# Moving the second pair's index scores and its top-256 select to later places in three quarters of a sparse-attention layer

## The chip, the cores and the metric

The kernel runs on one core of one Trainium2 chip. TensorE (PE) multiplies matrices into PSUM, its weight loads are shown apart (PEld), VectorE (DVE), ScalarE (ACT) and GpSimd (POOL) work on vectors, SyncE (SP) issues the DMAs. The metric is the device time of one execution in microseconds (us), lower is better.

## The reference, cut to what matters

Three layers over 2048 tokens of width 1024. The first two (gated linear attention and spatial gating, then retention and pooling) are not touched. The change lies in the third: all tokens are projected, and then two branches run beside each other, a gated delta rule in chunks of 64 and an attention in which every token sees only 256 chosen tokens.

```python
proj = h @ w_in[layer]
(qkv_a, z_a, b_a, a_a, q_b, ckv, z_b, iq, ik, iw) = jnp.split(proj, list(SPLIT_OFFSETS), axis=-1)
o_a = gated_deltanet(qkv_a, z_a, b_a, a_a, ...)
o_b = dsa_sparse_attention(q_b, ckv, iq, ik, iw, ...)
mix = jnp.concatenate([o_a, o_b], axis=-1) @ w_out[layer]
x = x + gate[:, None, :] * rmsnorm(mix, g_post[layer])

# in dsa_sparse_attention, for each block of 128 queries
rel = jnp.einsum('bqhd,bsd->bqhs', iqb, ik)                 # 8 index heads
score = jnp.einsum('bqh,bqhs->bqs', iwb, jax.nn.relu(rel))
score = jnp.where(key_pos[None, None, :] <= t[None, :, None], score, -jnp.inf)
_, sel = lax.top_k(score, k_top)                            # k_top = 256
...
p = jax.nn.softmax(logits, axis=-1)                         # over the chosen keys, 4 heads
return jnp.einsum('bqhk,bqkr->bqhr', p, kv_sel)
```

## The kernel before

**The quarters.** `layer2` (L972) walks over four quarters `q` of 512 tokens, each of four blocks `b` of 128 queries; block `i = 4q + b` sees `n = 128 (i + 1)` keys. The blocks form two pairs, (0, 1) and (2, 3). In the first quarter (`q = 0`) the first pair needs no select, since it sees at most 256 keys.

**What a quarter does.** `begin` (L1111) transposes the rows `x` into the tiles `xh` and `xl` and makes the first projections. `chains` (L1189) makes the other 28 projections, numbered 0 to 27: 24 matmuls of 512 columns into a `pj` bank each. Numbers 0 to 3 are the index queries, 4 to 11 keys and queries of the delta rule (each followed by a convolution on VectorE), 12 to 15 its values (the same), 16 to 27 queries and gates (ScalarE alone takes them out). `index_scores` (L1339) makes the scores of a pair in steps: two matmuls into an `ix` bank (L1355, L1356), a relu on ScalarE (L1362) and a multiply-add on VectorE (L1363), eight heads for each 512 keys. `select` (L1368) finds the 256th largest score of each query of a pair. It has seven rounds, in each of which VectorE counts for one block (L1400) and ScalarE for the other (L1406), and some dozen tiny VectorE instructions set the next threshold from both; then a search among the candidates (L1473 to L1483), two more counts, a repair by match-replace (L1513), and the masks `jd`, `ja`. It ends with two branches on a loaded flag (`tc.If`, L1532) for rare cases. `attention` (L1573) takes the blocks in turn and four heads in each: `setup` (L1588) copies the block's mask into `mk`, `scores` (L1600) makes three matmuls for each 512 keys (L1619) and adds the mask on VectorE (L1621), then comes an exponential (L1627), transposes (L1640) and products (L1650). `delta` (L1827) is a serial recurrence over the quarter's four groups of 128 tokens. `output` (L1299) multiplies both branches by the output weights (L210) and writes the rows.

**What sets the order.** The streams are Python generators. `weave` (L1077) takes steps from them in proportion to the weight that stands beside each, and `part(stream, wait, n)` (L1093) lets a stream wait for some steps and then gives `n` of it. `PARTS` (L46) says at which projections a quarter's three weaves begin and `PACE` (L45) holds weights. I call the three weaves A, B and C, and the last one, with `output`, the tail:

- A: projections 4 to 11 (to 10 in the last two quarters) with the first pair's index scores.
- B: projections to 19 (to 18) with the second pair's index scores and the first pair's select.
- C: projections to 27 with the second pair's select, after 4 steps of wait 10 steps of attention, and after 20 steps 6 of delta.
- tail: the rest of delta and of attention, then `output`.

Up to the end of C, TensorE's instructions stand in just this order (`manual_schedule`, L1040). On the other engines, and on TensorE in the tail, a scheduler orders them by program order and readiness when the kernel is built; on the chip every engine works down its own fixed list. Nothing moves across a `tc.If` in VectorE's list.

**Buffers that the change touches.** `row8` (L859) hands out tiles of 2048 columns by tags with few buffers. Tag `xh` (2 buffers) serves `xh` and later the delta branch's result `mhA`, `mlA`; tag `rb` (2 buffers) serves the score rows of the second pair and later the attention's result `mhB`, `mlB`. `output` reads `mhA` and `mlA` for the first half of each sum, `mhB` and `mlB` for the second.

Of the kernel before, what the change touches and what calls it, by code (L numbers as in the profile page):

```python
# [22 lines left out]
P = 128  # L23
# [18 lines left out]
ORDERED = '@@'  # L42


PACE = [(6, 3, 30, 30, 10, 40, 20, 6)] * 4  # L45
PARTS = [(4, 12, 20), (4, 12, 20), (4, 11, 19), (4, 11, 19)]  # L46


def f(ap):
# [12 lines left out]
class Builder:  # L62
# [794 lines left out]
        return self.sb.tile([P, TB if dt == F32 else 4 * TB], dt, tag=tag, bufs=1, name=self.nm(tag))  # L857

    def row8(self, name, dt=F32):  # L859
        pair = {"xr": "ra", "P": "ra", "score01": "ra", "xh": "xh", "wq": "xh", "mhA": "xh", "mlA": "xh"}.get(name)  # L860
        if pair:
            return self.big.tile([P, 2048], dt, tag=pair, bufs=2, name=self.nm(name))
        if name in ("score23", "mhB", "mlB"):
            t = self.big2.tile([P, 2048 + 8], dt, tag="rb", bufs=2, name=self.nm(name))
            return t if name == "score23" else t[:, :2048]
        return self.big2.tile([P, 2048], dt, tag="r8", bufs=4, name=self.nm(name))
# [105 lines left out]
    def layer2(self, src, dst):  # L972
# [65 lines left out]
        for q in range(NQ):  # L1038
            pace = PACE[q]
            with self.tc.manual_schedule(engines={mybir.EngineType.PE}):  # L1040
                st = self.begin(q, xn)
                x = PARTS[q]
                for _ in self.chains(q, st, range(1, x[0])):
                    pass
                n = [8 * sum(-(-(4 * q + b + 1) // 4) for b in pair if 4 * q + b >= 2) for pair in ((0, 1), (2, 3))]
                self.weave((self.chains(q, st, range(x[0], x[1])), 8 * (x[1] - x[0]) + pace[0]), (self.index_scores(q, st, (0, 1)), n[0]))
                self.weave((self.chains(q, st, range(x[1], x[2])), 8 * (x[2] - x[1]) + pace[1]), (self.index_scores(q, st, (2, 3)), n[1]),
                           (self.select(q, st, (0, 1)), pace[2]))
                att, delta = self.attention(q, st), self.delta(q, st)
                n = [4 * (1 + -(-max(0, i - 1) // 4) + 2 * -(-(i + 1) // 4)) for i in range(4 * q, 4 * q + 4)]  # L1050
                self.dtag = "ix"
                m = 8 * (28 - x[2])
                self.weave((self.chains(q, st, range(x[2], 28)), m), (self.select(q, st, (2, 3)), pace[3]),
                           (self.part(att, 4, pace[4]), 4 + pace[4]), (self.part(delta, pace[6], pace[7]), pace[6] + pace[7]))
            self.dtag = "pj"
            self.weave((delta, 40 - pace[7]), (att, sum(n) - pace[4]))
            if q + 1 < NQ:
                xn = self.load_rows(q + 1, src)
            self.output(q, st)
# [513 lines left out]
    def attention(self, q, st):  # L1573
# [5 lines left out]
        blocks, split = {}, []  # L1579
# [8 lines left out]
        def setup(b):  # L1588
            i = 4 * q + b
            n = (i + 1) * P  # L1590
            if b in st["masks"]:
                for u in range(0, n, 512):
                    m = min(512, n - u)
                    nc.scalar.activation(mk[:, u:u + m], st["masks"][b][:, u:u + m], AF.Copy, scale=-BIG)
            else:
                nc.gpsimd.memset(mk[:, :n], 0.0)
                nc.gpsimd.affine_select(out=mk[:, i * P:n], in_=mk[:, i * P:n], pattern=[[-1, P]], base=0, channel_multiplier=1,
                                        compare_op=ALU.is_ge, fill=-BIG)
# [103 lines left out]
        order = [(b, h) for b in range(4) for h in range(4)]  # L1702
        queries(0)
        setup(0)
        yield
        lag = 2 if q < 2 else 1
        for t, (b, h) in enumerate(order + [(4, h) for h in range(lag)]):
            streams = []
            if t >= lag:
                streams.append((values(*order[t - lag]), 2 * -(-(4 * q + order[t - lag][0] + 1) // 4)))  # L1710
            if b < 4:
                streams.append((scores(b, h), 3 * (1 + -(-max(0, 4 * q + b - 1) // 4))))
            if h == lag and b > 0:
                streams.append((after(b - 1), 3))
            yield from self.woven(*streams)
            if h == 2 and b < 3:
                queries(b + 1)
            if h == 3 and b < 3:
                setup(b + 1)
# [338 lines left out]
```

## Time and profile before

| what | before |
|---|---|
| median of 3 runs | 3370.99 us (3364.59 to 3376.85) |
| the profiled execution's own time | 3370.53 us |
| its span, first to last instruction | 3368.8 us |
| granted TensorE clock, mean | 0.971 |
| busy: PE, DVE, ACT, POOL | 94%, 57%, 36%, 32% |

The span is 1.7 us shorter than the execution's time; sums below are made against 3370.53 us. The third layer takes the second half of the span, from about 1648 us. [...] A busy TensorE is no TensorE at its peak: a matmul is counted from issue to its modelled end, so the spacing of matmuls is the better price.

### The profile page before, as it was taken

The numbers are of one execution on the slowest core, as the hardware profiler recorded it, in microseconds if no ns is written. First come the engines' busy times: TensorE is split into PE (matmuls) and PEld (weight loads), VectorE is DVE, ScalarE is ACT, GpSimd is POOL, SyncE is SP. The second block draws the span as 40 slices with busy tenths as digits, with TensorE's granted clock in tenths as the row PEclk, the third lists the DMA queues.
The fourth block names the chain that finished last, engine by engine and source line by source line (L and its number), as shares of the span: only waits on it lengthen the run. The fifth ranks groups of instructions, "written<-read, shape, count | busy, mean of one in ns | idle before, by whom it ended". The sixth has DMA issues, their size and how long they took to land. (4 is left out here: it accounts for less than half of the span.)

```text
span 3368.8 us, 45610 instructions
## 1 busy us (share of the span) xinstructions
PE 3171.5 (94%) x16546; PEld 2608.0 (77%) x16546; DVE 1912.2 (57%) x5082; ACT 1215.1 (36%) x2013; POOL 1071.8 (32%) x917
## 2 busy tenths in 40 slices
PE   8999999999999999999799899889998899986999
PEld 5878877778878787877687878779786787765887
DVE  2236456144514742144658647976588854898853
ACT  4222252212322323212233524444353452553552
POOL 4123262223653536352311221612126121134011
PEclk9999999999999999999899999999998999998999
DMA  4112247223545726212567555554545524434422
GB/s 124 34 45 94 101 138 254 66 69 116 172 128 191 255 98 225 81 38 88 175 215 238 172 191 186 182 174 146 179 156 163 159 92 167 147 119 141 150 64 72
DMA packets 380754, 472.33 MB, mean 140 GB/s; under 512 B 81251, under 2 KB 268851, under 8 KB 380502
## 3 DMA queue, kind: packets, MB, share of 16 engines
q1 hardware_dynamic: 380502, 469.20, 42.4%
q8 instruction: 130, 2.13, 0.3%
q14 instruction: 122, 1.00, 0.1%
HBM read 365.13 MB, written 103.99 MB: 139 GB/s over the span
## 5 line engine op out<-in xcount | busy, mean ns | idle before, releaser
L144 POOL TENSOR_TENSOR wl<-wr,wh 128x1024 fp32r<-128x1024 f32 x126 | 299.9, 2384 | 585.4 <-ACT wh L143 573.7
L210 PE MATMUL pj<-wh,xh 128*128 128x512 f32 x1024 | 402.9, 396 | 9.7 <-ACT wh L143 8.6
L210 PE MATMUL pj<-wl,xh 128*128 128x512 f32 x1024 | 404.1, 395 | 4.2 <-POOL wl L144 4.2
L199 PE MATMUL pj<-xh,wh 128*128 128x512 f32 x992 | 398.2, 402 | 7.7 <-ACT wh L143 5.2
L210 PE MATMUL pj<-wh,xl 128*128 128x512 f32 x1024 | 403.2, 394 | 0.0
L199 PE MATMUL pj<-xl,wh 128*128 128x512 f32 x992 | 394.0, 397 | 0.0
L199 PE MATMUL pj<-xh,wl 128*128 128x512 f32 x992 | 394.0, 397 | 0.0
L1202 PE MATMUL pj<-xl,wh 128*128 128x512 f32 x896 | 361.0, 403 | 10.3 <-DVE xl L165 5.6
L1202 PE MATMUL pj<-xh,wh 128*128 128x512 f32 x896 | 366.6, 409 | 0.2 <-PE pj L1202 0.2
L1202 PE MATMUL pj<-xh,wl 128*128 128x512 f32 x896 | 359.5, 401 | 0.0
L143 ACT CAST wh<-wr 128x1024 fp32r<-128x1024 f32 x126 | 130.5, 1038 | 434.8 <-PE pj L210 143.5
L210 PEld LDWEIGHTS pj<-wh,xh 128*128 128x128 f32 x1024 | 193.8, 189 | 52.8 <-ACT wh L143 9.4
L199 PEld LDWEIGHTS pj<-xh,wh 128*128 128x128 f32 x992 | 184.1, 186 | 60.7 <-ACT wh L143 7.0
L210 PEld LDWEIGHTS pj<-wl,xh 128*128 128x128 f32 x1024 | 193.9, 189 | 45.8 <-POOL wl L144 6.1
L210 PEld LDWEIGHTS pj<-wh,xl 128*128 128x128 f32 x1024 | 193.8, 189 | 40.5 <-issue 0.8
L199 PEld LDWEIGHTS pj<-xl,wh 128*128 128x128 f32 x992 | 184.0, 185 | 46.3 <-issue 4.5
L199 PEld LDWEIGHTS pj<-xh,wl 128*128 128x128 f32 x992 | 183.6, 185 | 45.9 <-issue 3.2
L1202 PEld LDWEIGHTS pj<-xl,wh 128*128 128x128 f32 x896 | 174.3, 194 | 48.2 <-DVE xl L165 8.3
L1363 DVE SCALAR_TENSOR_TENSOR score<-relu,iwc,score 128x512 f32<-128x512 f32 (+3 forms) x266 | 193.2, 727 | 32.1 <-ACT relu L1362 28.3
L1362 ACT ACTIVATE relu<-ix 128x512 f32<-128x512 f32 (+3 forms) x266 | 143.3, 543 | 185.0 <-PE ix L1356 124.8
L1202 PEld LDWEIGHTS pj<-xh,wl 128*128 128x128 f32 x896 | 173.4, 194 | 39.1
L1202 PEld LDWEIGHTS pj<-xh,wh 128*128 128x128 f32 x896 | 174.3, 194 | 36.6 <-PE pj L1202 1.3
(562 smaller groups left out, 6414.6 us busy)
## 6 DMA issues: line engine op xcount, KB each, us to landing
wh<-kh SPq DMA_DIRECT2D x140, 512.0 KB, 3.9
wl<-kl SPq DMA_DIRECT2D x140, 512.0 KB, 4.6
wr<-in_l_w_in_dram SPq DMA_DIRECT2D x92, 512.0 KB, 3.6
kh<-wh SPq DMA_DIRECT2D x37, 512.0 KB, 3.2
kl<-wl SPq DMA_DIRECT2D x37, 512.0 KB, 4.4
wr<-in_l_w_out_dram SPq DMA_DIRECT2D x32, 512.0 KB, 3.6
x<-y SPq DMA_DIRECT2D x32, 512.0 KB, 2.6
wr<-in_w_in_dram SPq DMA_DIRECT2D x29, 512.0 KB, 4.6
```

Of the source, the lines that this page charges most:

```text
L143: nc.scalar.copy(wh, raw)
L144: nc.gpsimd.tensor_tensor(out=wl, in0=raw, in1=f(wh), op=ALU.subtract)
L199: self.nc.tensor.matmul(ps[:m, :], a[:, k, :], b[tb][k], start=(n == 0), stop=(n == 3 * KT - 1))
L210: self.nc.tensor.matmul(ps, a[tb][k][:, o:o + P], b[:, k % 2, :], start=(n == 0), stop=(n == 3 * KT - 1))
L1202: nc.tensor.matmul(ps, a[:, k, :], b[0][k], start=k + n == 0, stop=k == KT - 1 and n == 2)
L1362: nc.scalar.activation(t[:, :m], ps[:, :m], AF.Relu)
L1363: nc.vector.scalar_tensor_tensor(out=o, in0=t[:, :m], scalar=w, in1=o, op0=ALU.mult, op1=ALU.add)
```

## The change

In the first quarter little changes: attention gives 4 steps in C instead of 10, later. In the other three quarters all of A, B and C now have eight projections:

- A: projections 4 to 11 with the first pair's index scores, as before.
- B: projections 12 to 19 with the first pair's select alone.
- C: projections 20 to 27 with the second pair's index scores; after 56 steps one step of attention, which loads queries and copies the first mask and has no matmul.
- tail: all of delta (40), all of attention, and the second pair's select (weight 80). `setup` of block 2 first runs whatever is left of that select (`st["late"]`).

The delta branch's result moves to tag `rb` and the attention's to tag `xh`.

```diff
-PACE = [(6, 3, 30, 30, 10, 40, 20, 6)] * 4
-PARTS = [(4, 12, 20), (4, 12, 20), (4, 11, 19), (4, 11, 19)]
+PACE = [(6, 3, 40, 30, 10, 80, 20, 6)] + [(6, 3, 40, 30, 56, 80, 20, 6)] * 3
+PARTS = [(4, 12, 20, 28), (4, 12, 20, 28), (4, 12, 20, 28), (4, 12, 20, 28)]
...
-        pair = {"xr": "ra", "P": "ra", "score01": "ra", "xh": "xh", "wq": "xh", "mhA": "xh", "mlA": "xh"}.get(name)
+        pair = {"xr": "ra", "P": "ra", "score01": "ra", "xh": "xh", "mhB": "xh", "mlB": "xh"}.get(name)
...
-        if name in ("score23", "mhB", "mlB"):
+        if name in ("score23", "mhA", "mlA"):
...
-                self.weave((self.chains(q, st, range(x[0], x[1])), 8 * (x[1] - x[0]) + pace[0]), (self.index_scores(q, st, (0, 1)), n[0]))
-                self.weave((self.chains(q, st, range(x[1], x[2])), 8 * (x[2] - x[1]) + pace[1]), (self.index_scores(q, st, (2, 3)), n[1]),
-                           (self.select(q, st, (0, 1)), pace[2]))
...
-                self.weave((self.chains(q, st, range(x[2], 28)), m), (self.select(q, st, (2, 3)), pace[3]),
-                           (self.part(att, 4, pace[4]), 4 + pace[4]), (self.part(delta, pace[6], pace[7]), pace[6] + pace[7]))
+                if q:
+                    self.weave(blocks(0), scores[0])
+                    self.weave(blocks(1), (chosen[0], pace[2]))
+                    self.weave(blocks(2), scores[1], (self.part(att, pace[4], 1), pace[4] + 1))
+                    early = 0
...
             self.dtag = "pj"
-            self.weave((delta, 40 - pace[7]), (att, sum(n) - pace[4]))
+            st["late"] = chosen[1]
+            self.weave((delta, 40 - early), (att, m), (chosen[1], pace[5]))
...
+            if b == 2:
+                for _ in st["late"]:
+                    pass
```

TensorE in C of the last quarter before, at the last projection but none: projections `pj`, delta on `ix` banks (L1900, L1906) and a transpose of the attention (L1640).

```order
L1202 MATMUL pj_30019<-xh_26444,wh_29915 128x512
L1202 MATMUL pj_30019<-xl_26446,wh_29915 128x512
L1202 MATMUL pj_30019<-xh_26444,wl_29916 128x512
L1900 MATMUL ix_30026<-ident,k_29944 128x128 x4
L1906 MATMUL ix_30035<-v_29942,Y_29940 128x128 x4
L1640 MATMUL tp_30041<-ident,P_29669 128x128 x4
```

The same place in the changed kernel, where every line number is 8 higher: the projection's three matmuls and then one step of the second pair's index scores (`ikH`, `ikL`).

```order
L1210 MATMUL pj_29590<-xh_26445,wh_29512 128x512
L1210 MATMUL pj_29590<-xl_26447,wh_29512 128x512
L1210 MATMUL pj_29590<-xh_26445,wl_29513 128x512
L1363 MATMUL ix_29637<-ikH,iq_26453 128x512
L1364 MATMUL ix_29637<-ikL,iq_26453 128x512
```

So attention and delta have left C on TensorE, and index scores have come in their place.

VectorE before, in the last quarter at the first delta step after the last projection (`vnew`, L1951): the second pair's select has done its rounds and searches candidates (`t_top`), and attention adds its mask (L1621).

```order
L1481 MAX t_m_5101_29740<-t_top_29739 128x8
L1951 TENSOR_TENSOR vnew_11743<-dt_29935,ix_30449 64x512
L1482 SCALAR_TENSOR_TENSOR t_m_5101_29740,t_vk_29738<-iota,t_eh_29411,t_m_5101_29740 128x16
L1477 MAX t_top_29811<-ja_5114_29813 128x8 x2
L1400 TENSOR_SCALAR jd_5131_29897,t_lt_29893<-score_4446_26642,t_vk_29738 128x1920
L1621 ISA P_29865,at_mx_29866<-ix_30814,near_29863 128x256
```

VectorE in the changed kernel, at the first steps of delta and attention after the last projection (`v`, L1898, and L1632): the same select is in its second round here (L1408 counts).

```order
L1632 ISA P_29755,at_mx_29756<-ix_29800,mk 128x384
L1632 ISA at_mx_29756 128x1
L1395 TENSOR_TENSOR t_t_29791<-t_t_29701,t_d_29786 128x2
L1898 TENSOR_TENSOR v_29743<-pj_29867,rin_29730 128x512
L1408 TENSOR_SCALAR jd_5103_29817,t_e_29816<-score_4446_26642,t_t_29791 128x1920
L1462 COPY t_t_29855<-t_t_29791 128x2
L1632 ISA P_29755,at_mx_29756<-ix_29811,near_29753 128x256
```

So nearly the whole second select now stands among the attention of the first pair and the first half of delta.

## Rows read from the trace of the kernel before

**Rows 1.** Stretches: from:to, length, busy PE, PEld, DVE, ACT, POOL; clock; DMA.

```profile
1697.00:1750.00 53.00, 52.76 (x273) 45.05 (x273) 29.75 (x74) 19.92 (x29) 13.40 (x10) 1.00 0.65 224
2030.00:2094.00 64.00, 64.00 (x334) 54.32 (x335) 47.18 (x119) 31.04 (x55) 14.16 (x12) 1.00 0.54 187
2094.00:2166.00 72.00, 66.38 (x309) 54.51 (x308) 65.09 (x218) 32.25 (x61) 40.84 (x67) 0.98 0.53 170
2166.00:2232.00 66.00, 56.61 (x260) 46.23 (x259) 51.81 (x241) 28.27 (x48) 18.45 (x27) 0.92 0.68 214
2232.00:2353.00 121.00, 111.38 (x835) 103.63 (x834) 85.17 (x271) 57.91 (x134) 30.73 (x31) 0.99 0.42 132
2422.00:2500.00 78.00, 77.25 (x387) 63.57 (x386) 65.81 (x158) 45.73 (x82) 15.24 (x13) 1.00 0.44 155
2500.00:2578.00 78.00, 72.44 (x323) 57.81 (x323) 69.84 (x207) 37.04 (x64) 44.56 (x67) 0.96 0.49 159
2578.00:2659.00 81.00, 58.64 (x262) 47.59 (x261) 64.41 (x257) 29.94 (x44) 19.68 (x25) 0.85 0.56 171
2659.00:2811.00 152.00, 145.35 (x1085) 136.59 (x1084) 97.83 (x311) 75.58 (x156) 30.64 (x32) 0.98 0.36 115
2878.00:2967.00 89.00, 85.69 (x417) 68.91 (x416) 79.29 (x174) 54.36 (x96) 15.34 (x13) 1.00 0.37 131
2967.00:3062.00 95.00, 83.81 (x351) 64.83 (x350) 86.16 (x225) 48.33 (x78) 55.01 (x82) 0.91 0.39 130
3062.00:3150.00 88.00, 61.17 (x274) 50.03 (x273) 71.48 (x242) 31.16 (x42) 10.09 (x8) 0.83 0.50 158
3150.00:3369.00 219.00, 200.27 (x1410) 182.96 (x1408) 124.16 (x358) 93.42 (x176) 32.05 (x34) 0.97 0.26 81
```

**Rows 2.** Waits of TensorE in C of the last quarter: total, times, longest.

```profile
PE ix L1619 <- DVE at_mx L1621: 21.5, 1, 21.5
PE ix L1619 <- ACT qh L164: 2.7, 1, 2.7
```

**Rows 3.** Timeline: matmuls of 128 columns in fp32, the last quarter's tail.

```profile
3257.52 1.06 PE L1650 MATMUL mm<-PT,ckvN 128*128 128x128 f32 x8
```

**Rows 4.** VectorE's groups by line, from 2878 to 3343 us: count, busy, mean.

```profile
L1363 DVE SCALAR_TENSOR_TENSOR score<-relu,iwc,score 128x512 f32<-128x512 f32 (+3 forms) x112 | 83.0, 742 | 9.0 <-ACT relu L1362 6.6 <-DVE score L1363 0.5
...
L1400 DVE TENSOR_SCALAR_CACHE_REDUCE jd<-score,t_t 128x1664 int8<-128x1664 f32 (+1 forms) x14 | 29.0, 2071 | 0.1
```

**Rows 5.** Waits of VectorE in C of the second quarter, and in the last tail.

```profile
DVE t_hi L1436 <- DVEq L1532: 9.6, 1, 9.6
...
DVE at_m L1625 <- DVEq L1532: 7.9, 1, 7.9
```

**Rows 6.** Timeline: second pair's select, first count and first mask copy; rounds between.

```profile
2162.94 1.15 DVE L1400 TENSOR_SCALAR_CACHE_REDUCE jd<-score,t_t 128x896 int8<-128x896 f32 x1
...
2261.84 0.52 ACT L1594 ACTIVATE mk<-jd 128x384 bf16<-128x384 int8 x1 [4.48 <-DVEq L1532]
...
3060.55 2.20 DVE L1400 TENSOR_SCALAR_CACHE_REDUCE jd<-score,t_t 128x1920 int8<-128x1920 f32 x1
...
3120.90 2.21 DVE L1400 TENSOR_SCALAR_CACHE_REDUCE jd<-score,t_t 128x1920 int8<-128x1920 f32 x1
...
3130.98 2.21 DVE L1400 TENSOR_SCALAR_CACHE_REDUCE jd<-score,t_t 128x1920 int8<-128x1920 f32 x1
...
3203.38 0.52 ACT L1594 ACTIVATE mk<-jd 128x384 bf16<-128x384 int8 x1 [4.70 <-DVEq L1532]
```

**Rows 7.** Timeline: the third quarter's start, output's last matmuls and the first cast.

```profile
2377.16 0.39 PE L210 MATMUL pj<-woh,mlA 128*128 128x512 f32 x1
...
2377.44 0.62 ACT L164 CAST xh<-jd 128x512 fp32r<-128x512 f32 x1 [18.63 <-POOL rmr L133]
...
2379.95 0.39 PE L210 MATMUL pj<-wh,mlB 128*128 128x512 f32 x1
```

**Rows 8.** Timeline: first pair's select in the last quarter, first count and mask copy.

```profile
2938.76 1.93 DVE L1400 TENSOR_SCALAR_CACHE_REDUCE jd<-score,t_t 128x1664 int8<-128x1664 f32 x1
...
3106.96 0.63 ACT L1594 ACTIVATE mk<-jd 128x512 bf16<-128x512 int8 x1 [12.10 <-DVEq L1532]
```

More of the change, by code (lines that the diff above doesn't have):

```diff
@@ L1045, in layer2 @@
                 n = [8 * sum(-(-(4 * q + b + 1) // 4) for b in pair if 4 * q + b >= 2) for pair in ((0, 1), (2, 3))]
-                self.weave((self.chains(q, st, range(x[0], x[1])), 8 * (x[1] - x[0]) + pace[0]), (self.index_scores(q, st, (0, 1)), n[0]))
-                self.weave((self.chains(q, st, range(x[1], x[2])), 8 * (x[2] - x[1]) + pace[1]), (self.index_scores(q, st, (2, 3)), n[1]),
-                           (self.select(q, st, (0, 1)), pace[2]))
+                blocks = lambda i: (self.chains(q, st, range(x[i], x[i + 1])), 8 * (x[i + 1] - x[i]))
+                scores = [(self.index_scores(q, st, pair), m) for pair, m in zip(((0, 1), (2, 3)), n)]
+                chosen = [self.select(q, st, pair) for pair in ((0, 1), (2, 3))]
                 att, delta = self.attention(q, st), self.delta(q, st)
-                n = [4 * (1 + -(-max(0, i - 1) // 4) + 2 * -(-(i + 1) // 4)) for i in range(4 * q, 4 * q + 4)]
-                self.dtag = "ix"
-                m = 8 * (28 - x[2])
-                self.weave((self.chains(q, st, range(x[2], 28)), m), (self.select(q, st, (2, 3)), pace[3]),
-                           (self.part(att, 4, pace[4]), 4 + pace[4]), (self.part(delta, pace[6], pace[7]), pace[6] + pace[7]))
+                if q:
[3 more added lines that the diff above has]
+                    early = 0
+                else:
+                    self.weave(blocks(0))
+                    self.weave(blocks(1), scores[1])
+                    self.dtag, early = "ix", pace[7]
+                    self.weave(blocks(2), (chosen[1], pace[3]), (self.part(att, pace[4], 4), 4 + pace[4]),
+                               (self.part(delta, pace[6], early), pace[6] + early))
+            m = sum(4 * (1 + -(-max(0, i - 1) // 4) + 2 * -(-(i + 1) // 4)) for i in range(4 * q, 4 * q + 4))
             self.dtag = "pj"
-            self.weave((delta, 40 - pace[7]), (att, sum(n) - pace[4]))
+            st["late"] = chosen[1]
+            self.weave((delta, 40 - early), (att, m), (chosen[1], pace[5]))
             if q + 1 < NQ:
```

## Prediction

> **What bounds the kernel now.** I read the stretches first, stage by stage for the three quarters that change [rows 1]: the first row is A of the first quarter, then A, B, C and tail of the second, third and fourth. Two things are to be seen. In A, B and C VectorE and TensorE are both nearly full, and the stages grow with the number of keys: 64, 72, 66 us in the second quarter, 78, 78, 81 in the third, 89, 95, 88 in the fourth. In the tails (121, 152, 219 us) TensorE is busy 91 to 96% and VectorE only 57 to 70%.
>
> Then I price TensorE by spacing, since busy time flatters it. Twelve matmuls of 512 columns lie between the two starts in [rows 7], 2.79 us, so 0.23 us each. Eight fp32 records of 128 columns take 1.06 us with their modelled end [rows 3]; I take 0.11 us each. An fp32 matmul leaves two records. By these prices and the counts of the order, A, B, C and tail hold at full clock 64, 63, 52, 108 us of TensorE work in the second quarter, 74, 67, 52, 143 in the third and 82, 73, 54, 195 in the fourth. Against the lengths, C loses 14, 29 and 34 us, B 9, 11 and 22, A up to 7, the tails 13, 9 and 24 (8 of that after the last matmul). Then the waits say who is late. In C of the last quarter TensorE waits 21.5 us in one piece for VectorE's first mask addition of the attention [rows 2]; VectorE has the first select's end, B's leftover and the second select's rounds before it. The clock row of C (0.92, 0.85, 0.83) is the same loss seen again: after such waits TensorE runs at the lower level for a while.
>
> So C is late because B overfills VectorE (second pair's scores and first select together) and attention then hangs on the first mask. The tail, in contrast, has VectorE to spare.
>
> **The change part by part.**
>
> *A.* It has the same kind of work. With eight projections it holds 192 x 0.23 = 44 us, 9 us of small fp32 matmuls, and the first pair's scores. For the last quarter that is 64 steps, 48 at full width (0.46 us for two matmuls) and 16 narrow ones, 25 us, so 78 us; 64 and 71 in the quarters before. The second pair's first steps leave A there. Before, A took 1.00, 1.05 and 1.09 times its work; VectorE was at 74, 84 and 89%. With VectorE relieved by eight steps of 0.7 us [rows 4] in the later two: **64, 74, 83 us** (before 64, 78, 89).
>
> *B.* Eight projections and 5 us of small matmuls, 49 us. TensorE now needs nothing from the select there, and the projections are taken out by ScalarE. The nearest row is A of the first quarter: eight projections with no scores beside them ran 53.0 us with 52.8 busy at full clock [rows 1]. So B goes at TensorE's pace: **50 us** each (before 72, 78, 95).
>
> *C.* Eight projections and the second pair's scores: 24, 40 and 56 full steps and 8 narrow ones, so 57, 65 and 72 us of TensorE work. VectorE has 32, 48 and 64 multiply-adds of at most 0.7 us, 21 to 45 us, and what is left of the first select, 10 to 20 us. It is no longer full, but in-order counts of 2.07 us [rows 4] stand between the multiply-adds, and the two branches at the select's end leave VectorE idle, 9.6 us in one case [rows 5]. With three quarters of such an idle time on TensorE in the longer stages and half in the short one: **60, 69, 80 us** (before 66, 81, 88).
>
> *Sum of A to C.* 174, 193, 213 instead of 202, 237, 272: 28, 44 and 59, together **131 us less**.
>
> *The tail* gets it back in part. By the order it holds 121, 152 and 206 us of TensorE work, that is 13, 9 and 11 more (six steps of delta and ten of attention, less what moved). The second block pair cannot start before the second select ends. Up to that point the order holds on TensorE 58, 75 and 91 us, behind it 63, 77 and 115. On VectorE, up to the same point, 69, 78 and 96 us: in the last quarter nine counts of 2.07 us, sixteen searches and their preparations, two match-replaces of about 2 us and some eighty tiny instructions, 46 us in all, and some 50 us of attention and delta. So the first half is VectorE's, and how full can it be? In C before, where the same select stood beside attention's first steps and the idle branches counted in, VectorE was busy 78, 80 and 81% [rows 1]. At 80%: 86, 98 and 120 us. The second half goes at TensorE's pace as tails did: 63, 78 and 118, and 8 us of end in the last quarter. Together **149, 176, 246 us** instead of 121, 152, 219: 28, 24 and 27, **79 us more**.
>
> The bounds of this first half come from the select's own span. Before, first count to first mask copy of the second pair took 99 us in the second quarter and 143 in the last [rows 6], 121 between by the mean. That included waiting for the first select. Unhindered rounds stood 5.0 us apart (two in 10.1 us); seven of them and the 72 us from the last round to the mask copy give 107 us, three quarters of 143; by the same share 74 and 91 in the other two. So the first half lies between 74, 91, 107 and 99, 121, 143. I take 86, 98, 120, near the middle, since in the tail the rounds have delta beside them, and no first select ahead.
>
> *Branches.* The same number is executed before and after, and each pair leaves VectorE idle 7.9 to 9.6 us [rows 5], which the 80% contains. [...]
>
> *The quarter's start.* `xh` of the next quarter reuses the buffers of the result that had tag `xh`. Before, that was delta's, read in the first half of each sum: the last matmul that reads it starts at 2377.16 us, and ScalarE's cast follows at 2377.44, while TensorE goes on until 2379.95 with the other half [rows 7]. Now it is attention's, read to the end. The cast, and all behind it on ScalarE and VectorE up to the first projection, comes 2379.95 - 2377.16 = 2.8 us later, and TensorE has nothing else then. Three starts: **8 us more**. Bounds: 0, if the projection's start waited for something else anyway, and 12 with the lower clock after it.
>
> *Nothing:* the first quarter (fewer steps of attention in C, as many more in the tail); buffer `rb`, since delta's first result is due at about 53% of delta and the select is through before; its casts only wait on ScalarE behind the mask copies.
>
> *Sum:* 3370.5 - 131 + 79 + 8 = 3326 us; the profiled execution stands 0.5 us under the median, so I keep **3326**.
>
> **The rivals.** This measurement can tell 0.3% from no change, 10 us; slower begins at 3381, faster ends at 3361.
>
> 1. *The tail goes at TensorE's pace.* The select runs unhindered and the first halves take 74, 91, 107 us: 35 us less than forecast, about 3290. For it: VectorE reached 91% in B of the fourth quarter. Against: there it had long rows of independent work, and a round of the select is a chain over VectorE and ScalarE.
>
> 2. *The second select starves the tail* (the other side). Its chain is no faster than before, 99, 121 and 143 us, because attention's exponentials and transposes stand between its counts on ScalarE and delta between them on VectorE. Then the tails are 59 us longer than forecast, 3385 us. TensorE, waiting in pieces, would also fall to the lower level as it did in C, and each percent of the clock in the first halves costs 2 us. It decides from first halves of about 98, 112 and 137 us on, where the tails have eaten the gain, and shows as slower from 102, 116 and 142. For it: TensorE's list has nothing else after the first pair. Against: half of the old span was waiting for the first select and B's leftover.
>
> 3. *The first select is late.* In the last quarter it took 168 us from first count to mask copy [rows 8], and B and C together will be 130. If it kept its pace the tail would start without a mask, 38 us late there and up to 11 in the third, so some 3370: no change. Against: it was slow because B's scores filled VectorE (86 of 95 us); now B has 38 to 43 us of VectorE work in 50.
>
> **How the numbers follow.** Forecast 45%, rival 1 20%, rival 2 20%, rival 3 10%, and 5% for C staying as long as it was, which would give 3326 + 26 = 3352. Faster by over 0.3%: forecast, rival 1, the last and a share of rivals 2 and 3 that stop short, 0.75. Within 0.3%: 0.13. Slower: 0.12. The range that leaves out 2 in 10 runs from 3280 (rival 1 with a full clock) to 3376 (between rival 3 and rival 2).
>
> **What would show it.** B at 50 us with a clock of 1.00 and no wait on TensorE; C at 60 to 80 us without the 21.5 us wait; in the tails a first half with VectorE at about 80%, its longest idle time at the branches, and TensorE waiting there for the mask addition or for delta's state; a wait of some 3 us more at three starts. The forecast is wrong if the mask copy of the second pair comes later than 116 us (mean) after the last projection, if TensorE's clock in the first half of the tails falls under 0.9, or if a multiply-add of the scores in C waits for the first select for more than 10 us.

## The result and the profile after

The changed kernel takes 3406.53 us (median of 4 runs, 3401.64 to 3409.6), the kernel before beside it 3370.53. The ratio is 1.0105 with a 95% interval of 1.0083 to 1.0127: 1% slower, where 3326 us was forecast and the range ended at 3376. The profiled execution has a span of 3405.0 us (before 3368.8), the mean granted clock fell from 0.971 to 0.963, and the engines' busy shares hardly moved (PE 94%, DVE 56%, ACT 35%, POOL 31%).

The stretches of the changed kernel answer to [rows 1], with the same columns: behind each busy time stands its number of instructions, and the clock is the mean granted share over the stretch. In the records of both traces, before and after, that share is either 1.00 or 0.50, and "the lower level" is 0.50. The rows are first the first quarter's tail, then A, B, C and tail of the second, third and fourth quarter.

```profile
1871.80:2001.50 129.70, 113.63 (x742) 100.71 (x740) 78.82 (x233) 45.05 (x121) 32.66 (x36) 0.96 0.51 162
2043.60:2108.00 64.40, 64.40 (x337) 54.80 (x338) 48.96 (x120) 31.61 (x57) 13.74 (x13) 1.00 0.55 183
2108.00:2157.00 49.00, 49.00 (x242) 41.41 (x241) 43.21 (x192) 17.44 (x32) 24.25 (x48) 1.00 0.74 242
2157.00:2222.60 65.60, 60.61 (x255) 49.15 (x254) 39.40 (x96) 22.47 (x42) 30.38 (x41) 0.95 0.56 176
2222.60:2380.50 157.90, 132.23 (x906) 121.41 (x905) 116.00 (x438) 70.14 (x161) 30.44 (x34) 0.89 0.41 126
2449.40:2522.90 73.50, 72.65 (x369) 60.69 (x370) 59.91 (x136) 39.67 (x71) 14.00 (x13) 1.00 0.47 162
2522.90:2572.90 50.00, 49.02 (x241) 41.44 (x240) 44.82 (x182) 20.38 (x32) 20.75 (x40) 1.00 0.68 221
2572.90:2659.70 86.80, 71.35 (x287) 55.63 (x286) 60.92 (x130) 31.39 (x57) 35.92 (x49) 0.92 0.47 146
2659.70:2853.00 193.30, 166.71 (x1160) 152.78 (x1159) 138.66 (x482) 92.62 (x181) 31.62 (x35) 0.90 0.34 104
2919.50:3004.60 85.10, 82.83 (x401) 67.56 (x402) 72.56 (x152) 47.67 (x85) 14.87 (x13) 0.98 0.41 140
3004.60:3057.00 52.40, 50.78 (x242) 42.65 (x241) 47.26 (x176) 23.41 (x32) 24.33 (x48) 0.97 0.69 223
3057.00:3154.70 97.70, 81.77 (x318) 61.75 (x317) 80.55 (x156) 41.35 (x72) 34.00 (x40) 0.91 0.39 124
3154.70:3405.00 250.30, 220.42 (x1492) 199.41 (x1491) 161.33 (x516) 114.24 (x201) 33.01 (x36) 0.92 0.26 81
```

B is what was promised: 49, 50 and 52 us with TensorE busy 97 to 100%. C and the tails are not. The clock is low in the rows where TensorE is busy least: rows with TensorE busy 97 to 100% have 0.97 to 1.00, rows with 82 to 92% have 0.89 to 0.96. It is 0.91 to 0.95 in C (0.83 to 0.92 before, so C kept part of that trouble), and 0.89 to 0.92 in the tails, which had been at 0.97 to 0.99. To compare stages exactly, the next table cuts both traces at the starts of the same projections; a tail here runs on to the next quarter's first projection.

| stage | before (2nd, 3rd, 4th quarter) | after | sum of changes | forecast |
|---|---|---|---|---|
| A | 64.5, 77.2, 89.1 | 64.4, 73.4, 85.1 | -8 | -10 |
| B | 71.6, 78.0, 95.3 | 49.0, 50.1, 52.4 | -93 | -95 |
| C | 65.9, 80.9, 87.2 | 65.6, 86.8, 97.7 | **+16** | -26 |
| tails and starts | 148.3, 176.8, 219.4 | 185.1, 217.9, 250.3 | **+109** | +87 |
| first quarter | 333.1 | 346.3 | **+13** | 0 |

With 0.5 us less in the rest this is the 36.2 us between the two spans. The forecast missed 42 us in C, 22 in the tails and 13 in the first quarter.

**The select's clock.** Four rows of the last quarter, to set beside [rows 6] and [rows 8]: the first select's last round, its mask copy, then the second select's first count and its mask copy. C is 3057.0 to 3154.7.

```profile
3051.61 1.95 DVE L1408 TENSOR_SCALAR_CACHE_REDUCE jd<-score,t_t 128x1664 int8<-128x1664 f32 x1
...
3111.54 0.63 ACT L1605 ACTIVATE mk<-jd 128x512 bf16<-128x512 int8 x1 [4.91 <-DVEq L1540]
...
3133.04 2.21 DVE L1408 TENSOR_SCALAR_CACHE_REDUCE jd<-score,t_t 128x1920 int8<-128x1920 f32 x1
...
3272.37 1.15 ACT L1605 ACTIVATE mk<-jd 128x512 bf16<-128x512 int8 x2 [10.12 <-DVEq L1540]
```

In the last quarter the rounds of the first select fill B to its end, and everything behind them, 55 us to the mask copy, lies in C; in the other two the last round begins 11 and 8 us ahead of B's end. The second select runs 139 us from first count to mask copy; before it was 143. In the other two quarters it is 100 and 124 (before 99 and 118). So moving it did not make it shorter. It begins later: 9, 16 and 22 us ahead of the last projection, where before it began 69, 80 and 89 us ahead (first counts at 2162.9, 2578.5 and 3060.6 against last projections at 2231.9, 2658.5 and 3149.4). And even that is only VectorE's first count. ScalarE's half of the first round needs the scores of the pair's second block, which are ready only with the end of C:

```profile
3158.11 2.00 ACT L1414 ACTIVATE ja<-score,t_t 128x2048 int8<-128x2048 f32 x1 [1.83 <-POOL score L1373]
```

It starts 3 us behind the last projection in all three quarters, and VectorE's second count 10, 12 and 13 us behind it. So six of the seven rounds and all that follows lie in the tail.

**The hole in the tail.** Three stretches around the second pair's first mask copy, one in each tail, and the stretch behind the first of them.

```profile
2282.00:2330.00 48.00, 27.76 (x165) 24.99 (x165) 33.63 (x122) 11.55 (x23) 7.57 (x8) 0.72 0.17 49
2330.00:2380.50 50.50, 50.14 (x331) 44.93 (x331) 28.92 (x91) 21.39 (x51) 13.74 (x15) 1.00 0.44 144
...
2730.00:2783.00 53.00, 30.44 (x175) 26.39 (x174) 37.12 (x118) 15.36 (x30) 7.63 (x8) 0.71 0.15 45
...
3244.00:3294.00 50.00, 30.66 (x168) 25.64 (x168) 32.49 (x91) 17.91 (x31) 6.42 (x7) 0.73 0.10 27
```

In the rest of these tails, as the first table cuts them, TensorE is busy 91 to 99% at a clock of 0.94 to 1.00. Inside the 48 to 53 us it is busy 57 to 61% at 0.71 to 0.73. What it does there, in the last quarter, the timeline of TensorE shows (in brackets the wait before, and for whom):

```profile
3253.08 1.80 PE L1917 MATMUL pj<-v,Y 128*128 128x128 f32 x8 [2.73 <-ACT on L1963]
3256.01 2.08 PE L1970 MATMUL pj<-vnew,kg 128*128 128x128 f32 x8 [1.13 <-ACT dt L1918]
3259.49 2.08 PE L1924 MATMUL pj<-Y,k 128*128 128x128 f32 x8 [1.40 <-DVE dS L1973]
...
3266.13 2.07 PE L1961 MATMUL pj<-dS,dt 128*128 128x128 f32 x8 [2.71 <-DVE kg L1914]
...
3277.34 0.80 PE L1630 MATMUL ix<-ckvH,qh 128*128 128x512 f32 x1 [5.54 <-DVE at_mx L1632]
```

Attention of the first pair is done, so only delta is left, and delta is a serial recurrence: in these rows its steps wait 1.1 to 2.7 us for VectorE or ScalarE. From 3253.5 us on the granted clock is 0.50 (the next view but one), and eight such records take 2.07 to 2.08 us instead of the 1.06 of [rows 3]. At 3277.34, 5 us after the mask copy, block 2 goes on, whose first two banks of scores had been filled by 3234. VectorE, which has to add the mask, has done nothing for 6.9 us before that: it stands at the two branches that end the second select (7.8 and 7.6 us in the other two tails).

```profile
3276.59 0.69 DVE L1632 CUSTOM_DVE_ANT_0 P<-ix,mk 128x512 f32<-128x512 f32 x1 [6.92 <-DVEq L1540]
```

The clock of two stretches dates the fall and the return:

```profile
3253.50:3280.50 27.00, 13.96 (x55) 11.80 (x55) 17.36 (x43) 6.83 (x12) 5.08 (x5) 0.50 0.11 32
3281.00:3330.00 49.00, 47.34 (x361) 43.45 (x361) 25.66 (x93) 30.14 (x57) 9.75 (x11) 1.00 0.17 49
```

So the clock is at 0.50 for 27 us, to some 3 us into block 2.

### The profile page after: what moved, and what is told of

It is laid out like the page before. It is cut to its first block, busy times and chain, and to the rows that moved or that the text cites. A ratio compares the mean times of both kernels' runs of the same rounds, so it can differ in the third digit from the quotient of the medians.

```text
span 3405.0 us, 45594 instructions
## 1 busy us (share of the span) xinstructions
PE 3191.8 (94%) x16546; PEld 2627.2 (77%) x16546; DVE 1916.6 (56%) x5082; ACT 1197.6 (35%) x1997; POOL 1053.1 (31%) x917
```

## The experiments

Times are medians, each beside runs of the kernel before on the same chip (3367.4, 3371.7 and 3369.3 us for the three groups of four). Stage lengths are cut as in the table above. The kernel before differs by up to 4 us between these groups and the first measurement (3370.5), so a difference in us between runs of two groups carries as much.

**e1: the first quarter's attention as before.**

```diff
-  (self.part(att, pace[4], 4), 4 + pace[4])        # first quarter's C: wait 10, give 4
+  (self.part(att, 4, pace[4]), 4 + pace[4])        # wait 4, give 10
-  self.weave((delta, 40 - early), (att, m), (chosen[1], pace[5]))
+  self.weave((delta, 40 - early), (att, m - (0 if q else pace[4])), (chosen[1], pace[5]))
```

> The changed kernel, but in the first quarter attention again waits 4 steps in C and then gives 10, as before the change. Theory (the tail of the first quarter, 115.3 us before and 129.7 after, is longer because attention starts later in C and has ten steps less done at its end): that tail goes back to some 115 us, and the time falls by about 14 us, to 3392 us. Rival (the tail is longer through the swapped tags or the order that the builder finds for the whole): it stays at 128 to 131 us and the time at 3406.

Measured: 3382.42 us, ratio 1.0040 (1.0025 to 1.0054). The first quarter's tail is 116.2 us again.

```profile
1866.30:1982.50 116.20, 109.27 (x729) 96.34 (x727) 74.56 (x224) 44.96 (x114) 30.50 (x33) 1.00 0.54 177
```

Its C is 62.3 us (after 66.1), so the edit gives 17 us in the two stages where it acts, and 24 in the time (21 when each is set against its own kernel before); the rest is spread over stages with the same code. "The first quarter: nothing" was wrong: the steps of attention that C gives later and fewer made the tail 13.5 us longer, and C did not become shorter for it. In the changed kernel the first quarter's clock in the tail was 0.96, which is 10 us at 0.50 and, by an estimate from the 1.06 and 2.08 us that eight records take at the two levels, at most 5 of the 13.5; which wait makes the rest is not shown.

**e2: the tags alone.** The kernel before, with the two lines on tags of the change.

> The kernel before with nothing but the tags of the two results swapped (delta's result in rb, attention's in xh). Theory, by the working of the prediction: the first cast of a quarter waits for output's last matmuls instead of its middle ones, 2.8 us at each of three starts, 8 us together, 3379 us. Rival (something else is late at that start, or the time before the first projection is filled): within 3 us of the kernel before. A third case: delta's result now waits for a score row of the second pair to come free, and the tails grow by more than 3 us each.

Measured, in five rounds: 3371.96 us, ratio 1.0011 (1.0002 to 1.0021), that is +1 to +7 us, 4.5 by the medians. The quarter's start, to compare with [rows 7]: TensorE's last two matmuls of the output and the first projection, and ScalarE's cast.

```profile
2380.14 0.39 PE L210 MATMUL pj<-wl,mhB 128*128 128x512 f32 x1
2380.37 0.39 PE L210 MATMUL pj<-wh,mlB 128*128 128x512 f32 x1
2381.30 0.50 PE L1202 MATMUL pj<-xh,wh 128*128 128x512 f32 x1 [0.54 <-ACT xh L164]
...
2380.62 0.62 ACT L164 CAST xh<-jd 128x512 fp32r<-128x512 f32 x1 [21.32 <-PE pj L210]
```

The cast does wait for the last matmul now. But before, it came 2.74 us ahead of the first projection, hidden by the output's last matmuls; now the projection follows it 0.68 us later. TensorE loses 0.93 - 0.23 = 0.7 us here and at the other two starts, not 2.8. The cast waits as forecast, but its price was set at the cast's delay and not at what TensorE loses by it.

**e3 and e5: the second select alone moved.** The second pair's scores stay in B beside the first select; e5 has the edit of e1 besides.

```diff
-  self.weave(blocks(1), (chosen[0], pace[2]))
-  self.weave(blocks(2), scores[1], (self.part(att, pace[4], 1), pace[4] + 1))
+  self.weave((self.chains(q, st, range(x[1], x[2])), 8 * (x[2] - x[1]) + 3), scores[1], (chosen[0], pace[2]))
+  self.weave(blocks(2), (self.part(att, pace[4], 1), pace[4] + 1))
```

> The changed kernel, but with the second pair's scores in B beside the first select, as before the change, so that only the select of the second pair is moved (to the tail); C holds eight projections and what is left of the first select. Theory (the select's move is what costs, the scores' move gains): A and B as in the kernel before (64 and 72, 77 and 78 to 82, 89 and 95 us), C at TensorE's pace since no multiply-add waits there, 52 to 58 us each, so A to C fall by some 14, 27 and 31 us; tails as in the changed kernel or up to 10 us shorter each, since the second select has its scores from the end of B on; sum about 3370 - 72 + 123 (the four tails) - up to 30 = 3390 to 3420 us. Rival (the tails grow because the scores come late, at the end of C): tails within 10 us of those before, and the time at 3310 to 3340 us.

> Both edits of the first two experiments that helped: only the select of the second pair is moved (its scores stay in B), and the first quarter's attention gives its ten steps in C as before the change. Theory (the two effects lie in different quarters and add): select alone gave 3347.8, the first quarter gives back 14 to 24 us, so 3324 to 3334 us, faster than the kernel before by 1.0 to 1.3%. Rival (the gain of the first quarter was partly that of another stage of that run): 3340 to 3348.

Measured: e3 3347.77 us, ratio 0.9939 (0.9925 to 0.9953), between the two ranges expected, and e5 3333.49, ratio **0.9891** (0.9870 to 0.9912), faster than both kernels. Against e1, which differs from e5 in the scores' place alone, the scores' move to C costs 1.5%, some 50 us. I had expected that move to be the gain and the select's to be the cost. B, C and tail of e5 in the last quarter:

```profile
2950.00:3052.80 102.80, 85.55 (x369) 64.48 (x368) 94.58 (x255) 53.81 (x88) 51.45 (x81) 0.97 0.39 123
3052.80:3096.10 43.30, 43.30 (x192) 35.86 (x191) 37.32 (x126) 16.49 (x23) 8.15 (x7) 1.00 0.74 243
3096.10:3333.70 237.60, 213.44 (x1490) 194.87 (x1488) 155.14 (x467) 106.74 (x194) 34.77 (x37) 0.95 0.28 87
```

B is long again, 102.8 us with VectorE at 92%. But C is eight bare projections, 43.4 us in the third and 43.3 in the fourth quarter, and takes the end of the first select and the beginning of the second there with TensorE busy throughout, at 1.00. In the second quarter C is 54.5 us: TensorE waits once, 8.3 us, for ScalarE to take out a projection, and ScalarE's list has stood 4.5 us at the first mask's copy, behind the branches. The second select begins 60, 39 and 49 us ahead of the last projection, and its mask copy comes 31, 86 and 99 us behind it (e1: 92, 105, 118).

**e4 and e10: projections as filling for the tail.** The last four projections go from C into the first third of the tail, in the changed kernel (e4) and in e5 (e10).

```diff
+  self.weave((self.chains(q, st, range(20, 24)), 32), scores[1], (self.part(att, 30, 1), 31))   # e10: no scores
+  rest = [(self.chains(q, st, range(24, 28)), 120)] if q else []
+  self.weave((delta, 40 - early), (att, m), (chosen[1], pace[5]), *rest)
```

> The changed kernel with the last four projections (24 to 27, gates of the attention branch, 22 us of matmuls) taken from C into the first third of the tail. Theory (in the first half of the tails TensorE waits in pieces for the second select and for additions, some 20 us, and loses some 17 us more at the lower clock level; C is not bound by TensorE's work but by VectorE's list): the tails grow by less than the 22 us that they get, 5 to 15 us each, with the low-clock time under 20 us; C falls by 8 to 18 us where VectorE bounds it; the sum is 0 to 30 us faster than the changed kernel, 3376 to 3406. Rival (the tails are bound by TensorE's order and not by gaps): tails grow by 20 to 25 us each, C falls by 22 in no quarter, and the time is 3406 to 3440.

> The kernel of experiment e5 (second select alone moved, first quarter as before) with the last four projections taken from C into the first third of the tail. Theory (in the last two quarters TensorE starts the tail with 3 to 9 us of work in the first 20 us, since the first mask comes only at the end of C and delta must load first; the projections fill this hole, while the select goes on by its own clock): third and fourth quarter C to end 10 to 15 us shorter each, second unchanged, 3303 to 3318 us. Rival (the second mask copy sets the second half, and what is filled ahead of it is lost behind it): within 8 us of e5, 3325 to 3341.

Measured: e4 3391.97 us, ratio 1.0074 (1.0060 to 1.0089), 15 us under the changed kernel (11 when each is set against its own kernel before) and within the range of the theory; but the last projection is itself moved, so the stages can't be told apart, and C and tail together fall by 6 and 9 us in the second and third quarter and by nothing in the fourth. e10 gave 3365.07, ratio 0.9984 (0.9975 to 0.9994): 30 us *slower* than e5, which neither side had. In the last quarter the second mask copy comes 157 us behind the end of B instead of 142 (92 instead of 86 in the second, 129 instead of 130 in the third), and C and tail together are 13, 2 and 17 us longer. Where the filling made the select later, the tail lost more than it gained. Which of its waits grows there I have not settled.

**e6: a short first select.** The search, the last counts, the repair and the two branches are left out.

```diff
+  if q and pair[0] == 0:            # after the rounds
+      lt = sm("t_lt")
+      for j in range(nb):
+          masks[pair[j]] = count(j, t, ALU.is_lt, lt, j)
+          yield
+      return
```

> The changed kernel with a short first select in the last three quarters: after its seven rounds the masks are taken at the last threshold; the search among candidates, the last counts, the repair and the two branches are left out, so the result is not the reference's. Theory (C is long because the second half of the first select stands between the scores' multiply-adds on VectorE): C falls from 65.6, 86.8, 97.7 us to TensorE's pace, 58, 66, 74, and the tails stay within 8 us, so the time falls by 40 to 60 us, to 3346 to 3366 us. Rival (C is bound by its scores alone, by relu on ScalarE and in-order banks): C stays within 8 us of what it is, the time at 3385 to 3407.

Measured: 3369.96 us, ratio 0.9999 (0.9986 to 1.0012), 4 us over the range of the theory. C is 57.5, 72.5 and 87.2 us:

```profile
2164.50:2222.00 57.50, 57.50 (x254) 47.34 (x253) 29.04 (x48) 19.94 (x36) 27.77 (x40) 1.00 0.65 202
2573.90:2646.40 72.50, 68.33 (x287) 55.59 (x286) 40.17 (x63) 28.43 (x50) 29.81 (x41) 0.95 0.57 174
3035.90:3123.10 87.20, 76.54 (x318) 61.02 (x318) 52.80 (x84) 36.12 (x64) 34.49 (x47) 0.94 0.47 145
```

That is 8, 14 and 11 us less, 33 of the 42 that the forecast of C missed. In the fourth quarter it stops 13 us above the 74 expected, and the waits of VectorE in that stretch say what stands there now:

```profile
DVE score L1371 <- ACT relu L1370: 22.3, 41, 1.7
DVE M L1839 <- POOL T L1836: 12.3, 2, 8.9
```

A copy of delta's preparation stands in VectorE's list and waits for GpSimd, 8.9 us in one case, with the multiply-adds queued behind it: the next thing late once the select is out of the way. The tails stay (183.6, 213.4, 249.7 us).

**e9: the first pair's select without its two branches.** With them go the repairs inside, of which the changed kernel runs two in these selects: one in the third quarter (2.4 us on VectorE), one in the fourth (3.4 us).

```diff
+  if pair[0] == 0:
+      yield
+      yield
+      continue
   with self.tc.If(flag(4 + j) != 0):
```

> The changed kernel without the two branches at the end of the first pair's select (the rare repair behind them is left out, so the result may differ where it is wanted). Theory (part of what keeps C long in the changed kernel is the end of the first select: around its two branches VectorE did 3.1 and 2.3 us of nothing in the last quarter and ran one repair of some 3 us, with the multiply-adds queued behind): C falls by 3 to 9 us in each of the three quarters, and the time by 10 to 25 us, to 3382 to 3396. Rival (the scores catch up later anyway, since behind the branches C goes at TensorE's pace): C within 2 us, the time at 3400 to 3408.

Measured: 3385.01 us, ratio 1.0049 (1.0032 to 1.0066), 22 us under the changed kernel (20 when each is set against its own kernel before). C falls by 3, 10 and 9 us, which is this sum. What a branch does to C in the changed kernel, VectorE's timeline in the last quarter shows:

```profile
3108.69 0.73 DVE L1367 TENSOR_SCALAR score<-ix,iwc 128x512 f32<-128x512 f32 x1
3112.50 0.07 DVE L1520 MEMSET score<- 128x8 f32 x1 [3.08 <-DVEq L1537]
...
3114.73 1.15 DVE L1400 TENSOR_SCALAR ja<-score,t_vk 128x1792 int8<-128x1792 f32 x1
3118.21 2.95 DVE L1371 SCALAR_TENSOR_TENSOR score<-relu,iwc,score 128x384 f32<-128x384 f32 x4 [2.32 <-DVEq L1542]
```

From 3109.4 to 3118.2 nothing is done for the scores: 3.1 us of waiting, 3.4 us of repair, 2.3 us of waiting; of the four multiply-adds that follow two had been ready, the first for 11.6 us (its relu ended at 3106.6).

**e7 and e12: the select's place in the order.** Weight 240 instead of 80, in the changed kernel and in e5.

> The changed kernel with weight 240 for the second select in the tail instead of 80, so that it stands ahead of most of delta and attention in the order. Theory (the second half of a tail hangs on the second select, whose instructions stand among those of delta and attention on VectorE): the second pair's first mask copy comes 75 to 105 us after the last projection instead of 91 to 118, the tails are 8 to 15 us shorter each, 3362 to 3382 us. Rival (the select's own chain sets its length, or delta behind it becomes late): mask copies within 6 us or the tails within 5 us of what they are, 3395 to 3415 us.

> The kernel of experiment e5 with weight 240 instead of 80 for the second select in the tail. In e7 the same edit moved no mask copy by more than 1 us, because there the select waited for its scores until the end of C. Here its scores are there at the end of B. Theory (the select's chain, not its place in the order, sets its length): mask copies within 4 us, time within 8 us of e5, 3326 to 3341. Rival (here the order matters, since the select can start in C): mask copies 8 to 20 us earlier in the last two quarters, 3305 to 3322.

Measured: e7 3405.65 us, ratio 1.0119 (1.0100 to 1.0138), mask copies within 1 us of the changed kernel's: the rival, as the select waits for its scores until the end of C. e12 gave 3344.36, ratio 0.9919 (0.9902 to 0.9935), 11 us behind e5, though the two intervals still touch: the copy came 8 us later in the second quarter, 3 us earlier in the third and 15 us later in the fourth. Neither expectation held; a higher weight bought nothing.

**e8: a short second select.** One round instead of seven, then the masks at that threshold, as in e6 but for the second pair; search, repair and branches are left out too.

> The changed kernel with a short second select in the last three quarters: one round and then the masks at that threshold; the other six rounds, the search, the repair and the branches are left out, so the result is not the reference's. Theory (the tails are 31 to 41 us longer than before because block 2 waits for the second select, half of it as gaps, half as the lower clock behind gaps): tails fall from 185, 218, 250 to TensorE's pace, 150, 184, 215 us, low-clock time from 34 to 38 us each to under 12, and the time to 3295 to 3325 us. Rival (delta's chain, now whole in the tail, sets the length): tails stay above 170, 205, 238 us, and the time above 3365.

Measured: 3312.05 us, ratio 0.9842 (0.9822 to 0.9862). The tails, cut as in the first table of stretches:

```profile
2221.90:2345.30 123.40, 119.00 (x909) 111.49 (x908) 83.64 (x265) 61.93 (x145) 32.02 (x35) 1.00 0.50 155
2626.30:2784.00 157.70, 154.74 (x1161) 144.55 (x1160) 96.28 (x297) 78.89 (x165) 32.12 (x35) 0.99 0.42 129
3085.90:3306.70 220.80, 209.32 (x1492) 192.09 (x1490) 115.06 (x333) 98.72 (x185) 32.91 (x36) 0.98 0.30 91
```

The same TensorE work, 35, 36 and 30 us shorter, with the clock at 0.98 to 1.00. Delta is whole in the tail here too, so delta alone is not what made the tails long: it was the second select. The run takes out three things of it at once, the late mask, its work on VectorE (which drops from 116, 139 and 161 us busy to 84, 96 and 115) and its two branches, and which of them cost how much was not tried apart. By the granted clock, time at the lower level is 34, 38 and 39 us in the tails of the changed kernel and 0, 3 and 7 here. How the loss divides into gaps and clock was not tried apart either. Eight records that take 1.06 us at 1.00 take 2.08 at 0.50; by an estimate from these two, at most half of the 34 to 39 us can be put down to the clock, 17 to 20 us in each tail, and TensorE is busy for only part of that time (13.96 of 27.0 us in 3253.5 to 3280.5).

**e11: six steps of delta back in C, in e5.**

> The kernel of experiment e5 with six steps of delta in C, as the kernel before had them. Theory (the hole at the start of the tail is filled by delta's first steps being done): 5 to 12 us shorter in the third and fourth quarter, 3310 to 3325. Rival (C is full on TensorE and grows by what the tail loses): within 6 us of e5, 3327 to 3340.

Measured: 3340.08 us, ratio 0.9909 (0.9892 to 0.9926), not to be told from e5. C grew by 22 and 16 us in the last two quarters, and the tails shrank by 24 and 8.

## Why the prediction was wrong

**What held.** B came out at 49, 50, 52 us (50 forecast), A at 64, 73, 85 (64, 74, 83). TensorE's work was counted well. The first half of the tail, up to the second pair's mask copy, took 91, 108 and 118 us against 86, 98 and 120, but that is in part luck: VectorE was busy for 78, 94 and 105 us there and not for 69, 78 and 96, and at 86 to 89% instead of 80%, and the two errors cancel.

**C, 42 us: the term that failed most.** The step that failed is the first select's part in C: the sum put "10 to 20 us" of it there, without a row, let TensorE idle for 3 to 8 us and charged nothing for the lower clock. The only price of a round that the prediction has is 5.0 us [rows 6]. In B the rounds share VectorE and ScalarE with the convolutions and came 4 to 13 us apart (12, 23 and 29 from the first, in A, to the second), and some 15, 25 and 34 us of VectorE's busy time went into C with the branches at the end. TensorE's waits in C come to 5, 15 and 16 us; in the last quarter they are

```profile
PE ix L1363 <- ACT relu L1370: 10.5, 10, 3.2
PE ix L1363 <- DVE score L1367: 5.4, 2, 4.0
```

and by the clock column it is at 0.50 for 7, 14 and 17 us, of which by the same estimate as in e8 at most half is lost. Together that is up to 8, 22 and 24 us, close to the 9, 22 and 26 that C (66, 87, 98) has over TensorE's work (57, 65, 72). Rival 3 had weighed the late first select, but only for the tail's first mask; the mask was there 37 to 43 us ahead of the tail, and the price fell on the multiply-adds that now stand behind the select. e6 and e9 show this: without everything behind the rounds C is 33 us shorter, without the branches and their repairs alone 22.

**The tails, 22 us: rival 2's mechanism, with a part that I priced at nothing.** The second select took 100, 124 and 139 us; rival 2 had 99, 121 and 143. The first halves came out near the forecast all the same, as 9 to 22 us of it lay in C. They were 5, 10 and -2 us off, the second halves 4, 8 and 7 us over, 31 together; the starts, put at 8 us and cheaper, make up most of the difference to the 22 of the table. What failed in the second halves is the step "at TensorE's pace". Cut at the mask copy, the halves read:

```profile
2222.60:2313.70 91.10, 70.79 (x498) 65.73 (x496) 78.48 (x313) 42.86 (x99) 11.54 (x13) 0.86 0.46 137
2313.70:2380.50 66.80, 61.44 (x408) 55.68 (x409) 37.52 (x125) 27.28 (x62) 18.90 (x21) 0.94 0.34 110
2659.70:2767.20 107.50, 87.06 (x626) 80.30 (x624) 93.63 (x341) 55.52 (x109) 11.69 (x13) 0.88 0.38 114
2767.20:2853.00 85.80, 79.65 (x534) 72.48 (x535) 45.03 (x141) 37.09 (x72) 19.94 (x22) 0.93 0.28 92
3154.70:3272.40 117.70, 102.37 (x738) 95.00 (x737) 104.53 (x349) 67.97 (x119) 11.78 (x13) 0.89 0.35 104
3272.40:3405.00 132.60, 118.05 (x754) 104.41 (x754) 56.79 (x167) 46.28 (x83) 21.23 (x23) 0.95 0.19 60
```

The first halves are at 0.86 to 0.89, under the 0.9 that the prediction had named as a sign of being wrong. Of its three signs two showed: this one, and a multiply-add in C that waited 11.6 us for the first select (10 was named; see e9). The mask copies came 105 us behind the last projection in the mean, where 116 was named. In the first halves the clock probably costs little, as VectorE, at 86 to 89%, is the fuller engine; that is argued and not tried. But the second halves start with block 2's first mask addition 4 us behind the copy and at the lower level (the clock is back at 1.00 some 8, 12 and 8 us behind the copy), and their 0.93 to 0.95 is, by the same estimate, at most 4 to 7 us each. The rival named the lower level, yet the forecast left it out.

**The first quarter, 13 us.** "Fewer steps of attention in C, as many more in the tail" was put at nothing without a row for it (e1).

**The starts.** 8 us were forecast; the trace shows 0.7 at each, and e2 measured 1 to 7 in all.

**Branches.** The prediction took 7.9 to 9.6 us of idle VectorE for each pair of branches, from two rows [rows 5]. In the trace of before, the six pairs of these three quarters have 5.8 to 9.6 us, so the two rows were the upper end; in the changed kernel it is 5.4 to 6.6 us at the first select's pairs and 6.9 to 7.8 at the second's. In e9, six branches fewer, with two repairs of 2.4 and 3.4 us inside them, are worth some 20 us.

The traces have no row of a branch alone; the idle times here hold all that such a block brings, and are what the sum had to go by.

**Two slips in the prediction's own numbers.** Rival 1's halves (74, 91, 107) lie 32 us under the forecast's and not 35, which makes 3294 and not 3290. Rival 2's 121 is a mean where the trace has 118. Neither moves the forecast.

**The deeper error** is in what I took the old B to be. It looked overfull, 95 us with TensorE's clock at 0.91, and the change took 93 us out of B. But B's overlap of the second pair's scores with the first select was what allowed the second select to begin 69 to 89 us ahead of the tail. The scores' move saved stage time and delayed the head of the longest serial chain by 60 to 67 us against the last projection. e5 keeps the overlap, and is 1.1% faster than the kernel before; against e1 the overlap alone is worth some 50 us.

## What to carry to other kernels

Before a producer is moved out of an overfull stage, follow the chain that starts from it. Here the second select took 99, 118 and 143 us before and 100, 124 and 139 after, so moving it did not shorten it, and what counted was when it could begin and how much independent work stood beside its end. A stage whose work on the bounding engine waits for little (bare projections, 43 us in two quarters of e5, 54 in the other) was here a better place for a latency chain than a stage that feeds its results through the same engine's list (C of the changed kernel, 66, 87 and 98 us, where in the last a multiply-add that was ready stood 11.6 us behind the select). And price a wait together with the clock that the trace shows beside it: here the tails with a hole of some 50 us at 0.71 to 0.73 were 30 to 36 us longer than without the select that made it.

## What was not expected of the hardware

In the holes TensorE never waited for more than 8.1 us at a time and was busy 57 to 61%, but the granted clock there was 0.71 to 0.73: 27 to 31 us at 0.50, of which some 3 us lay behind the start of block 2 in the last quarter. Before, tails with the same delta recurrence beside dense attention stayed at 0.97 to 0.99. The clock fell there without a long wait: in the third quarter's tail it fell from 1.00 to 0.50 at 2748.2 us, and no wait of TensorE in the 11 us before was over 2.3 us. The first select's six branches, which decide about rare cases, left VectorE idle for 18.4 us in C, with 5.8 us of repairs behind two of them, and taking all that out gave back some 20 us. The second select's six, none of which ran its repair, stand for 22 us of idle VectorE just ahead of block 2; no run leaves them out alone.
